# Four PSUM banks for one late feed-forward product, and a pacing copy that holds the cast of a weight chunk instead of its load

## The chip, the cores and the metric

The kernel runs on one core of a Trainium2 chip. The core has five engines with instruction streams of their own: TensorE (PE in the profile) multiplies matrices, VectorE (DVE), ScalarE (ACT) and GpSimd (POOL) work on elements, and SyncE (SP) issues nearly all DMAs here. Each works through its stream in order and waits at semaphores. The metric is the device time of one execution in microseconds, as the median of several runs.

## The reference

One layer of a hybrid decoder on 1024 tokens of width 1024, in float32. Cut to what matters here:

```python
h = rms_norm(x, attn_norm)
z = h @ w_in                          # convolution, q, six k/v groups, gates
conv_out = conv_mixer(a_conv, ...)    # GLU, causal depthwise conv, LayerNorm, swish
nsa_out = nsa_attention(q, kc, vc, ks, vs, kw, vw, gates)   # compressed + selected + window
x = x + concat([conv_out, nsa_out]) @ w_out
h = rms_norm(x, ffn_norm)
gate, up = split(h @ w_gate_up)
x = x + (silu(gate) * up) @ w_down    # width 2816
return rms_norm(x, final_norm)
```

## The kernel before

**Precision.** Every large product is done in three matmuls on fp32r operands. Each float32 operand is split into a rounded high part and the rest; high times high, high times rest and rest times high are added up. For weights this is `load_w` (line 220): a DMA brings a chunk of 512 KB into `w_raw`, ACT casts it into `w_hi` (line 230), and POOL subtracts the two into `w_lo` in four pieces (line 234). There are two buffers for `w_raw` and three each for `w_hi` and `w_lo`, taken in turn. So a load has to wait until POOL has subtracted the chunk two back, and a cast until PE has read the `w_hi` three back for the last time. `Feed` hands the chunks out in order; whoever takes one asks for the one two further on.

**Stages.** The tokens form two sets of 512. First the projections of the first half, the compressed branches and the convolution (to about 210 us). Then attention in two halves ("parts"): in the first (to about 420 us) the queries of the first four token tiles, in the second those of the last four. Attention alone can't fill PE, because each step is a chain: scores on PE (lines 851 to 855, tile `s`), minimum on DVE (859), exponential on ACT (866), the sum's reciprocal on DVE (870, 871, tile `l`), the gating on POOL (876, tile `pr`), a transpose on PE (882, `pt`), its split (240), and the product with the values on PE (910, 911, tile `o`). So `weave` emits a second stream, `fill_all`, between the steps of attention, by a ratio. In the first half this filling is `fill_b`: the second half's projections `zo` (queries and keys), `vo` (values) and `cv` (convolution), all through line 148, with 18 chunks of `w_in`. Then come the output projection of the first set (`wo`, line 1226) and its feed-forward, pair by pair of 128 columns: `gu` (line 1299), the activation `af`, its split `aw`, and `dn` (line 1324), whose sums DVE adds to the residual `x` (line 1327).

After attention, `second` (line 1626) does the same output projection for the second set (line 1250) and its norm, in which POOL scales rows and PE transposes them (line 261). The feed-forward of the first set goes on beside it, again by `weave`. After that the second set's feed-forward runs in a form with fewer products (line 1455).

**What sets the order.** The program emits one stream; a planner then orders each engine's instructions by a simulated time, with the program's order as priority, and adds the semaphores. An instruction that depends on nothing can thus come earlier on its engine than where it is written. Two things hold it:

- *The pace.* With `phase[0] == 0`, that is up to the end of attention's first half, `load_w` lets POOL copy one column of `l` of the attention step `PACE_B = 4` back (list `pace`) into the chunk's own buffer (line 225). What writes that buffer later must wait for the copy, and the copy for that step. In the second half `PACE_C` is 0 and there is no copy.
- *The banks.* The kernel divides PSUM into eight banks of 512 columns: five for the tag `x`, which `s` and `t` share, one for `o`, two for `z`. `next_bank` takes them in turn from a string of tags. The first set's feed-forward uses `FT` (line 1580), a list that holds "z" until `second` has been emitted and `ALL` afterwards (line 1649). It is read anew for each product, so a change takes effect from the next product that is emitted. In `second`, the output projection uses the first six tags of `ALL` ("stostt") and the transposes of the norm use `t`.

The feed-forward product that is emitted beside the norm of `second` is one `down_part`: eight sums of six matmuls each, 3 with the first half of `aw` and 3 with the second.

## Time and profile before

| | |
|---|---|
| median of 3 runs | 1441.14 us (1439.65 to 1441.8) |
| profiled execution | 1443.74 us, span 1442.0 us |
| granted TensorE clock, mean of the span | 0.994 |
| POOL copies of line 225 | 13, from 240.8 to 388.9 us |
| DMA, mean | 136 GB/s |

The span runs from the first to the last instruction; the execution's own time has some 2 us around it. Rows of the profile name an engine, a line of the program, the operation and the tiles (out<-in). Behind the second bar stands the idle time of the engine just before such an instruction, and what ended it. In the table of stretches, each engine's busy time stands beside the stretch's length; PEclk is the clock that TensorE was granted, as a share of full speed. Matmuls overlap: one of 512 columns is shown with some 0.39 us, though the next can start sooner.

### The profile page before, as it was taken

To read this page: it belongs to the slowest core of one execution; us is meant where nothing else is said; L and a number is where in the kernel's file an instruction comes from. 1 tells how busy PE (TensorE), PEld (TensorE's weight loads), DVE (VectorE), ACT (ScalarE), POOL (GpSimd) and SP (SyncE) were. 2 spreads that over 40 slices of the span, in tenths; PEclk is the share of its full clock that TensorE was granted. 3 is DMA by queue.
4 is the path that set the end of the run, shared out by engine and by line. 5 is a ranking of instruction groups with operands and counts; after the bars stand their busy time and mean duration, and the time that the engine had idled before them with its cause. 6 is when DMAs were issued, how large, how long until landed. Compare 5 with 4: busy or idle time off the path is not lost.

```text
span 1442.0 us, 23394 instructions
## 1 busy us (share of the span) xinstructions
PE 1410.9 (98%) x7941; PEld 1224.8 (85%) x7941; DVE 1031.6 (72%) x2306; ACT 763.7 (53%) x1593; POOL 739.4 (51%) x1043
## 2 busy tenths in 40 slices
PE   8999999999999999999999999999999999999997
PEld 7898888977788888888888888887788999999997
DVE  6487786777877859778697875231658987888884
ACT  6333566677865765666756654224325444445443
POOL 6467775766676656666666666546767000000001
PEclk9999999999999999999999999999999999999999
DMA  7246577665777343243343226723235333333421
GB/s 237 76 134 197 171 213 243 194 204 170 203 252 215 88 117 104 83 123 104 95 120 109 79 70 201 225 78 100 74 117 175 118 98 107 88 94 113 116 60 73
DMA packets 234119, 196.13 MB, mean 136 GB/s; under 512 B 13786, under 2 KB 204094, under 8 KB 233999
## 3 DMA queue, kind: packets, MB, share of 16 engines
q1 hardware_dynamic: 233854, 194.41, 44.9%
q8 instruction: 63, 1.03, 0.3%
q14 instruction: 58, 0.47, 0.1%
q10 hardware_dynamic: 144, 0.23, 0.0%
HBM read 160.85 MB, written 33.55 MB: 135 GB/s over the span
## 4 chain that ended last, share of the span: by engine, by line
PE 82%; DMA 5%; DVE 4%; POOL 4%; ACT 3%; issue 1%; SPq 0%; POOLq 0%; ACTq 0%; DVEq 0%
PE gu L1299 18%; PE dn L1324 16%; PE yy L1455 8%; PE pt L882 5%; PE zz L1455 4%; PE vo L148 3%; DMA w_raw<-in_w_in_dram 3%; PE cv L148 3%; PE wo L1250 3%; PE wo L1226 3%; PE o L911 3%; PE o L910 3%; POOL w_lo L234 3%; PE s L851 3%; PE zo L148 2%; PE aa L1455 2%
## 5 line engine op out<-in xcount | busy, mean ns | idle before, releaser
L234 POOL TENSOR_TENSOR w_lo<-w_raw,w_hi 128x256 fp32r<-128x256 f32 (+1 forms) x508 | 410.6, 841 | 169.1 <-ACT w_hi L230 162.5
L1299 PE MATMUL gu<-h,w_hi 128*128 128x512 f32 x768 | 252.5, 397 | 0.0
L1324 PE MATMUL dn<-w_hi,aw 128*128 128x512 f32 x690 | 242.0, 396 | 2.6 <-DVE aw L240 1.3
L230 ACT CAST w_hi<-w_raw 128x1024 fp32r<-128x1024 f32 (+1 forms) x147 | 152.7, 1049 | 171.6 <-PE gu L1299 72.3
L876 POOL TENSOR_SCALAR pr<-pr,l,gates 128x512 f32<-128x512 f32 (+5 forms) x192 | 144.7, 767 | 101.8 <-DVE l L871 86.0
L866 ACT ACTIVATE pr<-pr,m 128x512 f32<-128x512 f32 (+5 forms) x192 | 136.1, 709 | 94.9 <-DVE m L859 56.5
L1299 PEld LDWEIGHTS gu<-h,w_hi 128*128 128x128 f32 x768 | 143.4, 188 | 27.9 <-DVE h L240 0.2
L240 DVE TENSOR_TENSOR pl<-pt,ph 128x384 fp32r<-128x384 f32 x248 | 133.7, 550 | 45.7 <-ACT ph L240 38.7
L1542 POOL TENSOR_TENSOR rs<-rs,mhalf 128x1 f32<-128x1 f32 x4 | 3.3, 832 | 317.3 <-DVE rs L1541 317.2
L1324 PEld LDWEIGHTS dn<-w_hi,aw 128*128 128x128 f32 x690 | 129.3, 188 | 30.3 <-DVE aw L240 2.3
L1299 PE MATMUL gu<-h,w_lo 128*128 128x512 f32 x384 | 152.5, 397 | 0.0
L1327 DVE TENSOR_TENSOR x<-dn,x 128x512 f32<-128x512 f32 x177 | 118.6, 679 | 46.6 <-PE dn L1324 46.2
L240 ACT CAST ph<-pt 128x384 fp32r<-128x384 f32 x248 | 113.5, 474 | 60.7 <-PE pt L882 37.8
L1324 PE MATMUL dn<-w_lo,aw 128*128 128x512 f32 x345 | 136.2, 395 | 0.0
L882 PE MATMUL pt<-ident,pr 128*128 128x128 f32 x744 | 124.7, 274 | 2.5 <-DVE pl L240 1.3
L859 DVE CUSTOM_DVE_ANT_0 pr<-s,base 128x384 f32<-128x384 f32 (+3 forms) x192 | 101.0, 531 | 29.6 <-PE s L855 14.8
L148 PE MATMUL zo<-h,w_hi 128*128 128x512 f32 x320 | 107.7, 404 | 2.8 <-ACT w_hi L230 2.7
L882 PEld LDWEIGHTS pt<-ident,pr 128*128 128x128 f32 x744 | 93.3, 140 | 20.0 <-POOL pr L876 1.9
L1401 ACT CAST w_s<-sum 128x512 fp32r<-128x512 f32 x80 | 49.3, 621 | 113.9 <-PE yy L1455 94.3
L851 PE MATMUL s<-kt,q 128*128 128x384 f32 (+3 forms) x288 | 98.3, 343 | 2.8 <-DVE m L859 2.3
L1455 PEld LDWEIGHTS yy<-term,w_s 128*128 128x128 f32 x720 | 93.4, 188 | 5.4 <-DVE c L1470 0.3
L910 PE MATMUL o<-ph,vt 128*128 128x384 f32 x264 | 95.3, 361 | 1.9 <-DMA vt<-vs_d 0.9
(281 smaller groups left out, 3186.1 us busy)
## 6 DMA issues: line engine op xcount, KB each, us to landing
w_raw<-in_w_gate_up_dram SPq DMA_DIRECT2D x48, 512.0 KB, 3.9
w_raw<-in_w_down_dram SPq DMA_DIRECT2D x43, 512.0 KB, 3.5
w_raw<-in_w_in_dram SPq DMA_DIRECT2D x40, 512.0 KB, 4.6
u_raw<-in_w_gate_up_dram SPq DMA_DIRECT2D x20, 512.0 KB, 4.9
g_raw<-in_w_gate_up_dram SPq DMA_DIRECT2D x19, 512.0 KB, 4.0
q_d<-zh SPq DMA_DIRECT2D x12, 512.0 KB, 5.2
qc<-q_d SPq DMA_DIRECT2D x16, 384.0 KB, 4.6
pc_d<-pct SPq DMA_DIRECT2D x16, 384.0 KB, 3.2
```

What stands on the lines that cost most here:

```text
L148: lastpe[0] = pe.matmul(*args, **kw)
L230: act.copy(hi[:, :n], raw[:, :n])
L234: eng.tensor_sub(lo[:, q], raw[:, q], hi[:, q].bitcast(F32))
L240: pair = act.copy(hi, src), dve.tensor_sub(lo, src, hi.bitcast(F32))
L851: pe.matmul(sv, q2[0], kk_[:, 0, kk], start=True, stop=False)
L866: act.activation(pr[:, c0:n], pr[:, c0:n], AF.Exp, bias=m, scale=-1.0, accum_out=l3[:, r:r + 1])
L876: pool.tensor_scalar(x_, x_, l3[:, r2:r2 + 1], gates[:, i, c:c + 1], op0=ALU.mult, op1=ALU.mult)
L882: pe.transpose(pt[:, r * P:(r + 1) * P], prs[st][1 + r][:, kk * P:(kk + 1) * P], ident)
L910: pe.matmul(o[:, :384], v, ph, start=False, stop=False)
L1299: pe.matmul(o, w[:, k, :], h2[si][h][k // 4][:, k % 4, :], start=n == 0, stop=n == 3 * KT - 1)
L1324: pe.matmul(o, aws[si][:, a, k, t * P:(t + 1) * P], b[:, 0, h], start=n == 0, stop=n == 5)
L1455: pe.matmul(o, w[:, k, :], h[:, k, :], start=fresh and n == 0, stop=n == 11, skip_group_check=not fresh)
```

## The change

In `load_w`, the pacing copy writes a column of `w_hi` instead of `w_raw`. The DMA writes `w_raw`, so it no longer depends on the copy; the cast writes `w_hi`, so now it does. The copy itself no longer waits for `w_raw` to be free but for `w_hi`. In `second`, `FT` gets the tags z, s, z, o between the output projection and the norm, so the feed-forward products that are emitted from there to the end of `second` take their sums from four banks in turn (both of `z`, one of the five of `x`, and `o`) instead of two.

```diff
@@ load_w
         back = PACE_B if phase[0] == 0 else PACE_C
         if len(pace) >= back > 0:
-            pool.tensor_copy(raw[:, 0:1], pace[-back][:, 0:1])
+            pool.tensor_copy(hi[:, 0:1], pace[-back][:, 0:1])
         n = a * b
@@ second
         yield from out_proj_k(Feed(out_loads_k(p), 2), 1, ALL[:6])
+        FT[:] = "zszo"
         set_norm(1, p)
         yield from ffn_norm_in(1, "t", grow)
```

## The prediction

> **What bounds the kernel now.** I read the page first, for the busiest engine, then the stretches, for where that engine is idle, and then who waited for whom inside those stretches.

> ```profile
> span 1442.0 us, 23394 instructions
> ...
> PE 1410.9 (98%) x7941; PEld 1224.8 (85%) x7941; DVE 1031.6 (72%) x2306; ACT 763.7 (53%) x1593; POOL 739.4 (51%) x1043
> ```

> PE is busy for 98% of the span, so a change that leaves PE's work as it is can only win back PE's idle time and the time PE spends at a lower clock. The question is where these lie.

> ```profile
> core 0: us, PE busy (x) PEld busy (x) DVE busy (x) ACT busy (x) POOL busy (x), PEclk, DMA share, GB/s
> 210.00:420.00 210.00, 197.54 (x1143) 171.46 (x1142) 160.13 (x550) 152.19 (x466) 143.16 (x226) 0.97 0.68 210
> 322.00:330.00 8.00, 5.35 (x35) 4.34 (x33) 7.81 (x34) 5.07 (x15) 4.35 (x8) 0.98 0.94 289
> 330.00:337.00 7.00, 6.37 (x23) 5.62 (x24) 2.57 (x14) 5.02 (x21) 4.10 (x7) 0.53 0.31 107
> 382.00:391.00 9.00, 6.89 (x47) 5.88 (x46) 7.86 (x37) 7.21 (x23) 5.60 (x13) 1.00 0.78 219
> 391.00:395.00 4.00, 3.69 (x11) 2.96 (x12) 3.76 (x14) 3.95 (x17) 3.77 (x6) 0.57 0.84 232
> 418.00:422.00 4.00, 4.00 (x13) 3.54 (x13) 1.66 (x6) 1.55 (x5) 3.84 (x7) 0.57 1.07 401
> 420.00:880.00 460.00, 457.11 (x2457) 394.26 (x2456) 353.61 (x888) 283.12 (x524) 295.54 (x425) 1.00 0.40 112
> 1005.00:1023.00 18.00, 16.09 (x82) 12.25 (x81) 12.40 (x19) 10.97 (x17) 13.72 (x11) 1.00 0.11 30
> ```

> Attention's first half (210 to 420 us) has 210.00 − 197.54 = 12.5 us of idle PE; the second half, with twice the length, 2.9 us. Three short stretches show a granted clock of 0.53 to 0.57, and the two that follow a stretch with over 2 us of idle PE (8.00 − 5.35 and 9.00 − 6.89) lie where the change acts. The late feed-forward (1005 to 1023) has 18.00 − 16.09 = 1.9 us of idle. So the two parts of the change sit at the two places where PE still waits.

> Inside attention's first half, the groups by line show what ended PE's idle time:

> ```profile
> L148 PE MATMUL zo<-h,w_hi 128*128 128x512 f32 x112 | 39.5, 415 | 2.7 <-ACT w_hi L230 2.7
> L882 PE MATMUL pt<-ident,pr 128*128 128x128 f32 x186 | 32.7, 280 | 2.4 <-DVE pl L240 1.3 <-DVE m L859 0.4 <-POOL pr L876 0.4
> L851 PE MATMUL s<-kt,q 128*128 128x256 f32 (+3 forms) x79 | 26.2, 335 | 1.3 <-DVE m L859 0.8 <-PE o L910 0.5
> L148 PE MATMUL zo<-h,w_lo 128*128 128x512 f32 x56 | 23.4, 417 | 0.3 <-POOL w_lo L234 0.3
> L911 PE MATMUL o<-pl,vt 128*128 128x384 f32 x60 | 22.1, 368 | 0.5 <-DVE pl L240 0.5
> L910 PE MATMUL o<-ph,vt 128*128 128x384 f32 x60 | 21.7, 362 | 1.8 <-DMA vt<-vs_d 0.9 <-ACT ph L240 0.9
> L148 PE MATMUL cv<-h,w_hi 128*128 128x512 f32 x41 | 14.5, 419 | 1.6 <-ACT w_hi L230 1.6
> ```

> Weights end 2.7 + 0.3 + 1.6 = 4.6 us of it, attention's own steps 2.4 + 1.3 + 0.5 + 1.8 = 6.0 us.

> **The held load.** The copy of line 225 takes `l` of an earlier attention step into the buffer, and what it writes decides what is held.

> ```profile
> L225 POOL COPY w_raw<-l x13: 177/183/188, 240.8 to 388.9; 128x1 f32<-128x1 f32 x13
> ```

> It runs 13 times, so 13 chunks are touched. For two of them the order of time reads, on POOL, in the chain (the load's flight), on ACT and on PE:

> ```profile
> 323.86 0.18 POOL L225 COPY w_raw<-l 128x1 f32<-128x1 f32 x1
> ...
> 324.06 5.39 DMA w_raw<-in_w_in_dram
> ...
> 329.54 1.04 ACT L230 CAST w_hi<-w_raw 128x1024 fp32r<-128x1024 f32 x1 [2.49 <-DMA w_raw<-in_w_in_dram]
> ...
> 330.63 0.79 PE L148 MATMUL zo<-h,w_hi 128*128 128x512 f32 x1 [2.08 <-ACT w_hi L230]
> ```

> ```profile
> 382.71 0.18 POOL L225 COPY w_raw<-l 128x1 f32<-128x1 f32 x1
> ...
> 383.24 4.90 DMA w_raw<-in_w_in_dram
> ...
> 388.21 1.04 ACT L230 CAST w_hi<-w_raw 128x1024 fp32r<-128x1024 f32 x1 [1.44 <-DMA w_raw<-in_w_in_dram]
> ...
> 389.31 0.51 PE L148 MATMUL cv<-h,w_hi 128*128 128x512 f32 x1 [1.62 <-ACT w_hi L230]
> ```

> From copy to cast 329.54 − 323.86 = 5.7 us pass, and 388.21 − 382.71 = 5.5 us; nearly all of it is the load's flight. PE starts the moment the cast has ended.

> Afterwards the copy writes `w_hi`, so the load needs only a free `w_raw`, and the chunk is in the buffer when the copy runs. The cast can follow the copy directly: some 5 us earlier at these two places. The waits were 2.1 and 1.6 us, so both go, and with them the other w_hi and w_lo waits: **−4.6 us** (bounds 0 and −4.6).

> What else the step issues. It has the same 13 copies of 0.18 us, the same DMAs, casts and subtractions. SP's load moves ahead of attention's loads and stores in SP's queue; it then waits there for POOL's subtractions of the chunk two back instead of the copy, which stands behind those on POOL. Its traffic moves to a busy time: one wait for `vt`, 0.9 us, shows what a pushed transfer costs. I take 0, bounds −0.9 and +0.9. One more semaphore hop, from POOL to ACT, is not in the trace; the hop from POOL to SP is (324.06 − 323.86 − 0.18 = 0.02 us), and I take 0 again.

> The copy also gets a wait: for PE's last reading of the `w_hi` that is three chunks old. Queued behind it on POOL stand the gating of line 876 and the subtractions of line 234, for which PE waits. The tightest place before is here (the last matmul of the value chunks, then the copies for the two chunks that take their buffers):

> ```profile
> 268.48 0.29 PE L148 MATMUL vo<-w_hi,h 128*128 128x274 f32 x1
> ...
> 274.57 0.30 POOL L225 COPY w_raw<-l 128x1 f32<-128x1 f32 x2
> ```

> The buffer is free at 268.48 + 0.29 = 268.77, so 274.57 − 268.77 = 5.8 us before POOL gets to the copy. So the wait costs nothing in this order; the planner may choose another.

> **The clock.** The dips at 330 and 391 cost 7.00 × (1 − 0.53) = 3.3 us and 4.00 × (1 − 0.57) = 1.7 us. Each follows the stretch with a weight stall. If that idle time triggers them, they go too: **−5.0 us** (bounds 0 and −5.0). I take the whole, since both follow a weight stall within 2 us; the third dip, at 418, is not counted.
> [...]

> **Four banks.** For the product of the late feed-forward that runs beside the second set's norm, `FT` is "z", two PSUM banks. After the change products rotate over z, s, z, o: four.

> ```profile
> PE dn L1324 <- DVE aw L240: 1.1, 1, 1.1
> PE dn L1324 <- DVE x L1327: 0.5, 1, 0.5
> PE dn L1324 <- DVE rs L248: 0.2, 1, 0.2
> ...
> 1005.45 0.39 PE L1324 MATMUL dn<-w_hi,aw 128*128 128x512 f32 x1
> ...
> 1008.42 2.31 DVE L240 TENSOR_TENSOR aw<-af,aw 128x512 fp32r<-128x512 f32 x1 [1.88 <-ACT aw L240]
> ...
> 1010.78 0.50 PE L1324 MATMUL dn<-w_hi,aw 128*128 128x512 f32 x1 [1.14 <-DVE aw L240]
> ...
> 1023.31 22.26 PE gu L1299 x96
> ```

> A product is six matmuls, five of which don't need the late half of `aw` (DVE's, done at 1008.42 + 2.31 = 1010.73). With two banks PE has ten such matmuls; with four, twenty. One takes 22.26 / 96 = 0.232 us, so 10 more fill 2.3 us and cover the 1.1 us. The wait for `x` is for a bank whose sum DVE hasn't added yet; with two more banks it goes, and the 0.2 us too: **−1.8 us** (bounds 0 and −1.9, the stretch's whole idle time). The transposes of the norm share s's five buffers; the product takes at most one of them at a time, and I cost that at 0. Without that cover it is about one such 0.5 us wait. DVE does the same adds. Next late is the norm's own chain, which PE meets only at transposes, between feed-forward matmuls.

> **What is late next.** When weights come early, PE reaches attention's steps sooner, and their waits of 6.0 us can grow. At worst they take all 4.6 us; at best none, since earlier weights also give PE work while attention isn't ready. I take half, **+2.3 us**.

> **Sum.** −4.6 − 5.0 − 1.8 + 2.3 = −9.1 us. The profiled execution took 1443.74 us (span 1442.0), so it would take 1434.6. It lies 2.6 us above the median shown, 1441.14; from the median the forecast is **1432.0 us**. Its own range: with nothing given back and the `vt` wait saved 1441.14 − 11.4 − 0.9 = 1428.8; with all 4.6 us given back and one more `vt` wait 1441.14 − 6.8 + 0.9 = 1435.2.

> **The rivals.**
> *The dips stay.* The clock falls for another reason, or the idle time that remains suffices. The third dip stands behind a wait that isn't for weights:

> ```profile
> 417.25 0.74 PE L1226 MATMUL wo<-w_hi,mix 128*128 128x512 f32 x2 [1.86 <-DMA mix<-mix_d]
> ```

> For it speaks that 12.5 − 4.6 = 7.9 us of idle remain; against it that two of three dips stand behind a weight stall. Then −9.1 + 5.0 = −4.1: 1437.0 us. Chance 0.18. [...]
> *Attention takes over.* The first half runs at the pace of attention's softmax, of which the copies are the beat; weights that come sooner change only what PE waits for, and the clock falls as before. For: 6.0 us of waits there against 4.6. Against: PE is busy for 94% of that half and finds other work. Only −1.8 is left: 1439.3 us. Chance 0.20.
> *The load isn't early.* SP, in order, comes to it no sooner, because it stands behind waiting loads of attention, so the cast still follows a late landing. Again 1439.3 us. Against: the buffer of the load of 324.06 was free over 20 us earlier, when POOL had subtracted the chunk two back:

> ```profile
> 297.18 2.83 POOL L234 TENSOR_TENSOR w_lo<-w_raw,w_hi 128x256 fp32r<-128x256 f32 x4
> ```

> Chance 0.06.
> *POOL is held, and it is slower.* The planner moves the copy forward on POOL by more than the 5.8 us, or PE is that much later there than planned; POOL then stands in front of the gating, and PE waits for transposes. One such stall priced like the one at 330 is 2.1 + 3.3 = 5.4 us. It decides once POOL holds PE as long as weights do now (9.6 us with the dips, so nothing is won there) and one stall more: 5.4 − 1.8 = +3.6, 1444.7 us. For: the new order isn't known, and the copy's new wait stands on the engine that serves both attention and the weights. Against: 5.8 us is the tightest place of the 13. Chance 0.14.

> **How the numbers follow.** The forecast has 0.42. A measurement of this kernel can tell 0.2%, 2.9 us, from no change. Faster by more: the forecast 0.42, two thirds of the dips' case (its 4.1 us is little above 2.9) 0.12, and a quarter of the two 1439.3 cases 0.06: 0.60. Slower by more: the POOL case, 0.14, and 0.02 of the rest, 0.16. Same: 0.24. The range leaves out half of the POOL case and as much at the fast end: 1428 to 1444.

> **What would show it.** Right: line 225's group reads `w_hi<-l`; the casts follow it within 1 us; waits of zo and cv for w_hi are gone from PE's list; the granted clock in the stretches after 322 and 382 is 1.00; the late product's waits for `aw` and `x` are gone. Wrong: casts that still end with a wait for the DMA (the load isn't early); POOL's idle time before line 225 ended by PE (POOL held); the same idle sum in 210 to 420 under other names (attention takes over); dips without weight stalls.

## The result and the profile after

The changed kernel takes 1431.33 us (median of 4 runs, 1430.44 to 1432.28) against 1441.47 us of the kernel before in the same session (4 runs): 0.9934 [0.9916, 0.9952], 10.1 us less. Taken once more in a later session, under the label changed_again, it took 1428.43 us (6 runs) against 1441.76 (26 runs): 0.9915 [0.9897, 0.9933]. The forecast was 1432.0 us, with a range from 1428 to 1444.

The head of the page and the stretches that the prediction showed, now of the changed kernel (columns as there; at the end of a line the granted clock, the DMA share and GB/s):

```profile
span 1430.6 us, 23380 instructions
...
PE 1406.5 (98%) x7941; PEld 1224.0 (86%) x7941; DVE 1030.7 (72%) x2306; ACT 762.7 (53%) x1593; POOL 738.6 (52%) x1043
```

```profile
210.00:420.00 210.00, 203.09 (x1184) 177.57 (x1183) 165.10 (x566) 154.48 (x475) 145.84 (x229) 0.98 0.73 225
322.00:330.00 8.00, 7.65 (x45) 6.55 (x46) 7.77 (x31) 5.49 (x16) 7.50 (x12) 1.00 0.87 282
330.00:337.00 7.00, 7.00 (x45) 6.14 (x44) 5.14 (x22) 6.15 (x27) 4.21 (x8) 1.00 0.41 114
382.00:391.00 9.00, 9.00 (x52) 7.91 (x51) 8.47 (x27) 7.82 (x27) 7.13 (x12) 1.00 0.70 216
391.00:395.00 4.00, 4.00 (x22) 3.38 (x21) 3.88 (x13) 3.93 (x12) 4.00 (x7) 1.00 0.40 89
239.00:243.00 4.00, 3.96 (x15) 3.86 (x16) 2.38 (x10) 3.21 (x12) 4.00 (x10) 0.57 0.48 179
409.00:414.00 5.00, 5.00 (x16) 4.04 (x17) 3.37 (x9) 2.57 (x7) 3.74 (x6) 0.66 1.06 408
420.00:880.00 460.00, 457.08 (x2458) 393.81 (x2457) 353.78 (x890) 283.72 (x523) 298.60 (x427) 1.00 0.39 109
1005.00:1023.00 18.00, 18.00 (x92) 14.94 (x91) 12.10 (x18) 8.02 (x11) 12.00 (x13) 1.00 0.28 80
```

PE's idle time in attention's first half fell from 12.5 to 210.00 − 203.09 = 6.9 us, and in the late product from 1.9 to nothing. The second half is as it was (2.9 us). The dips at 330 and 391 are gone. There is a new one at 239, and the one of 418 is now at 409.

The groups of PE in the same first half (matmuls by line and tile; behind the second bar the idle time before them):

```profile
L148 PE MATMUL zo<-h,w_hi 128*128 128x512 f32 x141 | 46.8, 400 | 0.2 <-ACT w_hi L230 0.2
L882 PE MATMUL pt<-ident,pr 128*128 128x128 f32 x213 | 36.1, 276 | 0.8 <-DVE m L859 0.4 <-POOL pr L876 0.2
L851 PE MATMUL s<-kt,q 128*128 128x128 f32 (+3 forms) x95 | 31.9, 344 | 0.6 <-DVE pl L240 0.5
...
L911 PE MATMUL o<-pl,vt 128*128 128x384 f32 x69 | 25.4, 368 | 0.3 <-DVE pl L240 0.3
L910 PE MATMUL o<-ph,vt 128*128 128x384 f32 x69 | 24.8, 359 | 1.0 <-ACT ph L240 0.9
L148 PE MATMUL cv<-h,w_hi 128*128 128x512 f32 x64 | 21.3, 399 | 0.0
...
L1226 PE MATMUL wo<-w_hi,mix 128*128 128x512 f32 x27 | 10.3, 436 | 2.4 <-DMA mix<-mix_d 2.4
...
L905 PE MATMUL o<-pct,vcs 128*128 128x384 f32 x15 | 5.9, 396 | 1.4 <-DVE ou L915 1.4
```

Waits for weights: 4.6 us before, 0.2 now. Attention's own waits: 6.0 us before; now 0.8 + 0.6 + 0.3 + 1.0 and a new 1.4 at line 905, 4.1 us. The wait for `mix`, which the change doesn't touch, went from 1.9 to 2.4 us.

Why weights are no longer late, in the order of time (SP's queue, then POOL, ACT and PE), for the first of the two chunks that the prediction followed:

```profile
295.40 0.55 SPq L229 DMA_DIRECT2D w_raw<-in_w_in_dram  x1
```

```profile
324.25 0.18 POOL L225 CAST w_hi<-l 128x1 fp32r<-128x1 f32 x1
324.66 1.05 ACT L230 CAST w_hi<-w_raw 128x1024 fp32r<-128x1024 f32 x1
...
325.77 0.49 PE L148 MATMUL zo<-h,w_hi 128*128 128x512 f32 x1 [0.23 <-ACT w_hi L230]
```

Its load is issued 28.9 us ahead of the copy. The cast follows the copy by 0.4 us instead of 5.7, and PE waits 0.23 us instead of 2.08.

**Where the time went, stretch by stretch.** Idle time and clock don't add up to time by themselves, so I also compared the traces matmul by matmul: the n-th matmul of each line and tile in one against the n-th of the same in the other, and the median difference of their starts in a stretch of 40 us. Negative is earlier than in the profiled execution of the kernel before:

```
us, against before       from 160   from 440   from 960  from 1040   at the end
changed kernel               +0.6       -8.3       -8.3      -11.4        -11.5
the same, later session      +0.2      -12.2      -12.2      -15.3        -15.3
```

From 160 to 440 us, that is across attention's first half, the changed kernel gains 8.9 us. Idle time makes 12.5 − 6.9 = 5.6 of it. The clock makes 3.3: three dips before lost 3.3 + 1.7 + 1.7 = 6.7, two dips now lose 4.00 × (1 − 0.57) = 1.7 and 5.00 × (1 − 0.66) = 1.7. Together 8.9; that the two add up to the tenth is chance, since a stall can cost more than the idle time shown, as in the late product below (1.31 us for 1.14). The second half neither gains nor loses, and the late product brings 3.1.

### The profile page after: what moved, and what is told of

It is laid out like the page before. It is cut to its first block, busy times and chain, and to the rows that moved or that the text cites. A ratio compares the mean times of both kernels' runs of the same rounds, so it can differ in the third digit from the quotient of the medians.

```text
span 1430.6 us, 23380 instructions
## 1 busy us (share of the span) xinstructions
PE 1406.5 (98%) x7941; PEld 1224.0 (86%) x7941; DVE 1030.7 (72%) x2306; ACT 762.7 (53%) x1593; POOL 738.6 (52%) x1043
## 4 chain that ended last, share of the span: by engine, by line
PE 89%; DVE 4%; DMA 3%; POOL 2%; ACT 2%; issue 1%; SPq 0%; POOLq 0%; ACTq 0%; DVEq 0%
PE gu L1299 19%; PE dn L1324 17%; PE yy L1455 8%; PE zo L148 6%; PE pt L882 5%; PE zz L1455 4%; PE vo L148 3%; PE zc L148 3%; PE wo L1250 3%; PE wo L1226 3%; PE o L911 3%; PE o L910 3%; PE s L851 3%; PE cv L148 2%; PE aa L1455 2%; PE s L855 2%
## 5 line engine op out<-in xcount | busy, mean ns | idle before, releaser
L234 POOL TENSOR_TENSOR w_lo<-w_raw,w_hi 128x256 fp32r<-128x256 f32 (+1 forms) x508 | 409.9, 839 | 157.4 <-ACT w_hi L230 152.2
L1299 PE MATMUL gu<-h,w_hi 128*128 128x512 f32 x768 | 253.1, 397 | 0.0
L1324 PE MATMUL dn<-w_hi,aw 128*128 128x512 f32 x690 | 240.9, 395 | 0.7 <-DVE af L1306 0.3
L230 ACT CAST w_hi<-w_raw 128x1024 fp32r<-128x1024 f32 (+1 forms) x147 | 152.5, 1050 | 163.4 <-PE gu L1299 61.1
L876 POOL TENSOR_SCALAR pr<-pr,l,gates 128x512 f32<-128x512 f32 (+5 forms) x192 | 144.8, 767 | 97.1 <-DVE l L871 86.9
L240 DVE TENSOR_TENSOR pl<-pt,ph 128x384 fp32r<-128x384 f32 x248 | 133.4, 549 | 52.9 <-ACT ph L240 44.5
L1299 PEld LDWEIGHTS gu<-h,w_hi 128*128 128x128 f32 x768 | 143.4, 188 | 27.7 <-DVE h L240 0.2
L1324 PEld LDWEIGHTS dn<-w_hi,aw 128*128 128x128 f32 x690 | 129.4, 188 | 27.2 <-DVE af L1306 0.9
L1299 PE MATMUL gu<-h,w_lo 128*128 128x512 f32 x384 | 152.5, 397 | 0.0
L1327 DVE TENSOR_TENSOR x<-dn,x 128x512 f32<-128x512 f32 x177 | 118.3, 679 | 47.2 <-PE dn L1324 46.7
L240 ACT CAST ph<-pt 128x384 fp32r<-128x384 f32 x248 | 112.9, 474 | 53.3 <-PE pt L882 29.4
L1324 PE MATMUL dn<-w_lo,aw 128*128 128x512 f32 x345 | 136.2, 395 | 0.0
L882 PE MATMUL pt<-ident,pr 128*128 128x128 f32 x744 | 123.9, 273 | 0.9 <-DVE m L859 0.4
L859 DVE CUSTOM_DVE_ANT_0 pr<-s,base 128x384 f32<-128x384 f32 (+3 forms) x192 | 100.7, 530 | 22.3 <-PE s L853 14.3
L882 PEld LDWEIGHTS pt<-ident,pr 128*128 128x128 f32 x744 | 93.5, 140 | 17.7 <-issue 1.3
L148 PE MATMUL zo<-h,w_hi 128*128 128x512 f32 x320 | 105.6, 399 | 0.5 <-DVE pct L720 0.3
L851 PE MATMUL s<-kt,q 128*128 128x384 f32 (+3 forms) x288 | 98.7, 346 | 2.1 <-DVE m L859 1.5
L911 PE MATMUL o<-pl,vt 128*128 128x384 f32 x264 | 94.8, 359 | 0.9 <-DVE pl L240 0.9
```

Of the source, the lines that this page charges most:

```text
L148: lastpe[0] = pe.matmul(*args, **kw)
L230: act.copy(hi[:, :n], raw[:, :n])
L234: eng.tensor_sub(lo[:, q], raw[:, q], hi[:, q].bitcast(F32))
L240: pair = act.copy(hi, src), dve.tensor_sub(lo, src, hi.bitcast(F32))
L851: pe.matmul(sv, q2[0], kk_[:, 0, kk], start=True, stop=False)
L876: pool.tensor_scalar(x_, x_, l3[:, r2:r2 + 1], gates[:, i, c:c + 1], op0=ALU.mult, op1=ALU.mult)
```

## The experiments

The changed line and the line of the banks can be set one at a time, and the pace can be moved. Three readings of the gain in attention's first half were set against each other:

- **A, earlier is better.** PE gains because weights reach it sooner. Whatever releases the casts still earlier gains more, whatever releases them later loses.
- **B, ACT.** A cast that waits on ACT for its landing load holds attention's exponentials and splits behind it in ACT's stream; the gain is ACT's time.
- **C, the flight.** The copy set the right moment, but the load's flight (5.39 and 4.90 us in the prediction's two rows) stood between it and PE. What takes the flight out of that path gains, whichever tile is held.

In the list of waits from 235 to 396 us, ACT's rows for the held casts and for attention's exponential read, before and in the changed kernel (us, times, the longest):

```profile
ACT w_hi L230 <- DMA w_raw<-in_w_in_dram: 10.9, 7, 3.4
ACT pr L866 <- DVE m L859: 9.5, 15, 2.3
```

```profile
ACT pr L866 <- DVE m L859: 18.5, 19, 2.6
...
ACT w_hi L230 <- DMA w_raw<-in_w_in_dram: 2.2, 1, 2.2
...
ACT w_hi L230 <- POOL w_hi L225: 1.5, 2, 0.8
```

ACT stands at the casts for 2.2 + 1.5 = 3.7 us instead of 10.9, but 9.0 us longer in front of the exponential, for DVE's minimum. All waits in that list add up to 38.5 and 35.2 us, so on the whole ACT was freed by little.

All kernels were compared with the kernel before in their own session (medians 1440.96, 1441.76 and 1441.83 us, 25 to 29 runs each). "In place" is the gain from 160 to 960 us in the comparison by matmuls; that profile of the kernel before lies about 2 us above its median, which makes these some 2 us too good. The last two columns are PE's idle time in that one profile: from 210 to 420 us, attention's first half, and from 420 to 880 us, where no copy runs in any of them. In the kernel before they are 12.5 and 2.9 us, in the changed kernel's first profile 6.9 and 2.9.

```
                                       us      ratio [95%]             in place  idle 1st  2nd
cast alone                          1436.44   0.9966 [0.9952, 0.9979]    -6.7      8.0     3.2
banks alone                         1439.92   0.9994 [0.9977, 1.001]     +0.8     13.4     2.5
load held, a step earlier           1437.09   0.9975 [0.996,  0.9989]    -5.6      8.2     4.5
cast held, a step later  (3 back)   1430.4    0.993  [0.9909, 0.9952]   -10.3      7.0     3.2
cast held, two later     (2 back)   1444.12   1.0016 [1.0003, 1.0029]    +2.8     13.6     4.4
cast held, a step earlier (5 back)  1451.61   1.0057 [1.0032, 1.0082]   +12.1     19.8     3.8
nothing held                        1446.88   1.0032 [1.0016, 1.0049]    +4.0      7.9    10.7
both held, load one step earlier    1438.25   0.997  [0.9958, 0.9983]    -2.8      7.9     4.9
both held, load two steps earlier   1436.32   0.9955 [0.9939, 0.9971]    -2.7      8.2     6.4
first two chunks not held           1439.94   0.9985 [0.997,  1.0001]    -2.7     12.4     2.9
changed kernel, again               1428.43   0.9915 [0.9897, 0.9933]   -12.4      6.1     2.9
```

### The parts alone

```diff
 cast_alone, against the changed kernel
-        FT[:] = "zszo"
 banks_alone, against the kernel before
+        FT[:] = "zszo"
```

> Only the pacing copy is changed (it writes w_hi); the late feed-forward keeps its two z banks. Theory A (what counts is how early a chunk's weights are ready against attention's progress): the whole gain but the banks' share, the measured 0.66% of the changed kernel less 1.8 us of idle time, so 7 to 8 us faster than before; the stretch around 1000 to 1020 us again shows 1.5 to 2 us of idle PE. Rival (the gain comes from the late product, and the first half only swaps its waits): under 3 us.

> Only FT is set to z, s, z, o; the copy still writes w_raw. Theory A: the first half of attention is as before (12.5 us of idle PE from 210 to 420 us, 4.6 us of it for weights), the late product's 1.8 us of waits are gone: 1.5 to 2 us faster than before. Rival as above: 5 us or more.

The cast alone brings 4.9 us (0.9966 of 1441 us; the interval, 0.9952 to 0.9979, is 6.9 to 3.0 us), less than the 7 to 8 that A expected. The banks alone can't be told from no change by the time: −0.9 us [−3.3, +1.4]. In place they can. In the comparison by matmuls, the step from 960 to 1040 us is −3.08 us for banks_alone, and −3.07 or −3.08 in all eleven profiles of this study with four banks; for cast_alone, the only other one with two, it is 0.00. So the banks are worth 3.1 us, more than the 1.5 to 2 expected, and scatter elsewhere can hide it: at 960 us, ahead of anything that the banks touch, banks_alone stood 2.4 us behind the kernel before in these two executions.

The stretches of the late product in cast_alone and in banks_alone show the idle time of it:

```profile
1000.00:1023.00 23.00, 21.32 (x105) 16.86 (x106) 16.50 (x22) 11.13 (x17) 18.72 (x17) 1.00 0.16 47
```

```profile
1000.00:1023.00 23.00, 23.00 (x109) 18.91 (x108) 12.11 (x20) 12.17 (x19) 17.32 (x16) 1.00 0.19 55
```

In the kernel before the idle time of this stretch is 1.9 us, but the gain is 3.1. The starts of matmuls tell why:

```profile
1009.24 0.40 PE L1324 MATMUL dn<-w_lo,aw 128*128 128x512 f32 x1
1010.78 0.73 PE L1324 MATMUL dn<-w_hi,aw 128*128 128x512 f32 x2 [1.14 <-DVE aw L240]
```

From one start to the next 1.54 us pass where 0.23 would do, so this stall costs 1.31 us; the profile gives 1.14 as idle, since the matmul before it is shown as busy for its whole 0.40 us. The matmul behind this stall also took 0.34 us until the next one started (1010.78 to 1011.12), instead of 0.23. Added up over the starts from 998 to 1026 us that lie more than 0.30 us apart, what exceeds 0.23 us comes to 3.1 us in the kernel before and to 0.2 in banks_alone.

cast_alone has the changed kernel's instruction order up to 1000 us, too. Its profile stands within 0.9 us of the changed kernel's up to 650 us, and then loses 2.1 us at one late minimum of attention, which the changed kernel's profile doesn't show:

```profile
655.59 0.55 PE L882 MATMUL pt<-ident,pr 128*128 128x128 f32 x3 [0.88 <-DVE m L859]
```

The two parts thus add up to 4.9 + 3.1 = 8.0 us, against 10.1 and 13.3 for the whole change. What is missing to the first lies within the intervals. What is missing to the second doesn't quite: by the ratios it is 12.2 ± 2.6 us against 4.9 ± 1.9 and 3.1. A stall in one profile can't explain a median of twelve runs, so the cause of the rest stays open. The changed kernel's own two profiles stand 3.9 us apart from 410 us on.

### The load a step earlier, the cast a step later

```diff
 load_5, against the changed kernel
-PACE_B = 4
+PACE_B = 5
-            pool.tensor_copy(hi[:, 0:1], pace[-back][:, 0:1])
+            pool.tensor_copy(raw[:, 0:1], pace[-back][:, 0:1])
 cast_3, against the changed kernel
-PACE_B = 4
+PACE_B = 3
```

> The copy writes w_raw again, so it holds the load, but takes the column of five attention steps back instead of four (PACE_B = 5), with the four banks. A step of the first half lasts some 200/32 = 6.2 us, about the 5.5 us that the load takes from copy to cast. Theory A: weights are ready about as early as in the changed kernel, so 7 to 10 us faster than before, with under 1.5 us of PE waits for w_hi. Theory B (the gain comes from ACT no longer standing still for a landing, 10.9 us before, with softmax queued behind it): ACT still waits 8 to 12 us for DMAs, and the time is within 4 us of before.

> The changed kernel with PACE_B = 3: the cast is held, but by an attention step one later. Theory A: weights are ready some 6 us later, about as late as before the change; PE waits 3 to 6 us for weights again, and only the banks and little more are left: 1 to 4 us faster than before. Theory B: ACT waits for no landing here either, so 7 to 10 us faster.

load_5 leaves the flight where it was and only moves it one step of attention ahead. It gains 3.9 us of which the banks are 3.1, and ACT still stands at seven casts:

```profile
ACT w_hi L230 <- DMA w_raw<-in_w_in_dram: 8.0, 7, 3.1
```

By its time alone that is B's forecast. The stretches say where the time lies, attention's first half and the second:

```profile
210.00:420.00 210.00, 201.82 (x1183) 175.90 (x1183) 163.35 (x562) 155.48 (x473) 144.39 (x228) 0.99 0.71 221
420.00:880.00 460.00, 455.49 (x2447) 391.27 (x2446) 357.25 (x888) 283.54 (x527) 294.64 (x426) 1.00 0.38 108
```

In the first half PE's idle time fell to 8.2 us, most of the way to the changed kernel's, with one dip in place of three; in the comparison by matmuls load_5 gains 9.0 us from 160 to 440 us, the changed kernel 8.9. It falls behind in the second half, where no copy runs, with 4.5 us of idle against 2.9 and 3.4 us lost from 440 to 960 us. So where the copy acts, a load released one step earlier did about as well in this execution as taking the flight out of the way, while ACT still waits 8.0 us at casts against 10.9. That speaks against B, and it doesn't tell A from C.

cast_3 frees its casts later than the changed kernel, the 13 copies by 3 to 12 us (6 in the middle), and is just as fast: 0.993 against 0.9934 and 0.9915. PE waits 1.8 us for its weights from 235 to 396 us, where A expected 3 to 6. None of its casts waits for anything:

```profile
L230 ACT CAST w_hi<-w_raw 128x1024 fp32r<-128x1024 f32 (+1 forms) x14 | 14.6, 1051 | 0.0
```

A falls here: with the flight out of the way, later by a step loses nothing.

### How much hold, and the changed kernel again

```diff
 no_pace, cast_2 and cast_5, against the changed kernel
-PACE_B = 4
+PACE_B = 0      (2, 5)
 both_held, and both_2 with 2 for 1
+        if len(pace) >= back + 1 > 1:
+            pool.tensor_copy(raw[:, 0:1], pace[-back - 1][:, 0:1])
 free_first
-        if len(pace) >= back > 0:
+        if len(pace) > back + 2 > 2:
```

> The changed kernel with PACE_B = 0: no copy at all, neither the load nor the cast is held. Theory C (what cost time is that the load's flight lay between the copy and the cast, where ACT, POOL and PE stand in a planned order and meet a landing later than planned): the flight is out of the path here too, ACT waits under 4 us for landings of w_in, PE under 1 us for weights; within 4 us of the changed kernel. Theory A (the earlier the weights the better) wants it at least as fast as the changed one. Rival (the hold itself is worth something, because it spreads the projections over attention's steps): 5 us or more slower than the changed kernel, with attention's waits on PE up.

> The changed kernel with PACE_B = 2: the cast is held by two steps more than in the changed kernel, some 12 us. Theory C: lateness alone does no harm as long as the planner knows it, since PE's order puts attention first; within 4 us of the changed kernel, ACT's waits for landings near 0. Theory A: weights are 6 us later than before the change, PE waits over 5 us for them, slower than before or like it.

> The changed kernel with a second copy: w_hi is held by the column of four steps back as in the changed kernel, and w_raw by that of five steps back. The load is late again, by all but one step of some 6 us, but the flight of about 5 us is still covered. Theory C: as fast as the changed kernel within 3 us, ACT's waits for landings of w_in under 4 us. Rival D (what helps is that SP can send the loads far ahead, freeing its queue): most of the gain is lost, 3 to 6 us slower than the changed kernel.

> The changed kernel, measured beside the following ones. 8 to 11 us faster than before; its time is what the other three are compared with.

Without any hold the kernel is slower than before. Its weights are never late, but PE takes the projections too early and has too few left at the end of the half, where attention's chain is alone:

```profile
420.00:460.00 40.00, 31.63 (x161) 24.66 (x162) 33.91 (x127) 30.04 (x90) 21.06 (x30) 0.90 0.60 170
```

8.4 of the 10.7 us in the table's last column stand there; the changed kernel has none (40.00 of 40.00 busy). So the hold itself is worth 1446.88 − 1428.43 = 18.5 us (both from one session), as the rival said. This is the second blow to A, and C's forecast, within 4 us of the changed kernel, fails with it. The changed kernel itself gained 13.3 us here, somewhat more than the 8 to 11 expected. cast_2, with the casts two steps later, is slower than before as well, 15.7 us behind the changed kernel where C allowed 4. PE waits for weights only 0.8 us from 235 to 396 us, where A expected over 5; 10.9 us it waits there for attention's steps and loads. That the late casts leave it too little to do beside them fits this, but no run shows it by itself.

both_held lets the load go one step ahead of the cast instead of at will. ACT's waits for loads are then 5.6 us (10.9 before), and it gains 3.5 us, about what the banks bring, so it is 9.8 us slower than the changed kernel, where C allowed 3. That a load is only a step ahead is not enough to cover it.

> As both_held, but w_raw is held by the column of six steps back, two before that of the cast. Some 12 us lie between, where in both_held six of the pairs of copies were under 5 us apart. Theory C (the landing between copy and cast is what costs): ACT's waits for landings of w_in under 3 us, within 3 us of the changed kernel. Rival D (the loads must be free altogether, or what both_held lost it lost by its other order in the second half): again 6 to 10 us slower than the changed kernel, with those waits under 3 us all the same.

> The changed kernel with PACE_B = 5: the cast is held by an attention step one earlier. Theory A (the earlier the better): 1 to 3 us faster than the changed kernel. From the kernel without a copy, which was 18 us slower than the changed one because PE had no projections left at the end of the first half (8.4 us of idle PE from 420 to 460 us): slower by 0 to 5 us than the changed kernel.

> The changed kernel, but the first two chunks (the value weights) are not held; the other 11 are. In the changed kernel PE stands still for 2.1 us between 235.7 and 238.4 us with these weights not yet cast, and the clock is 0.5 for 3.4 us behind it. If the hold of these two is what starves PE there: that stall gone, 2 to 4 us faster than the changed kernel. Rival (the hold is worth something for every chunk, as the kernel without any showed): the stall comes back later, 0 to 5 us slower than the changed kernel.

With two steps ahead the flight is covered:

```profile
ACT w_hi L232 <- DMA w_raw<-in_w_in_dram: 1.0, 1, 1.0
```

and PE waits for no weights in that stretch. By B and by C this kernel should be as fast as the changed one. It is 5 to 8 us slower (0.9955 against 0.9934 and 0.9915; the intervals overlap with the first, not with the second). Both halves of attention again:

```profile
210.00:420.00 210.00, 201.78 (x1172) 177.04 (x1171) 164.37 (x559) 152.96 (x469) 146.57 (x241) 0.98 0.70 218
420.00:880.00 460.00, 453.56 (x2438) 391.71 (x2438) 357.01 (x883) 283.87 (x524) 291.22 (x424) 1.00 0.38 109
```

In the first half its idle time, 8.2 us, is 1.3 to 2.1 us above the changed kernel's two profiles; in the second it is 6.4 us against 2.9, where neither a load nor a cast is held. So in this execution the larger part of what it lacks lies where the change doesn't act, as one form of rival D had it; both_held shows the same, with 7.9 and 4.9 us.

cast_5 is the clearest miss. It differs from the changed kernel by one step, and it is 20 to 23 us slower by the medians (18 to 20 by the ratios). PE's waits (from 235 to 396 us):

```profile
PE o L905 <- DVE ou L915: 4.6, 2, 2.6
PE zo L148 <- ACT w_hi L230: 2.7, 2, 2.1
PE o L910 <- ACT ph L240: 1.7, 3, 0.9
PE s L855 <- DMA kt<-ks_d: 1.6, 1, 1.6
```

PE waits 12.4 us for attention's own steps and loads there (15.1 in all, of which weights are 2.7), more than three times the changed kernel's 3.4. POOL is not the cause: no idle time stands before its copies.

```profile
L225 POOL CAST w_hi<-l 128x1 fp32r<-128x1 f32 x12 | 2.1, 188 | 0.0
```

free_first leaves the two value chunks at 241 us without a hold, because PE stands still in front of them in the changed kernel (4.00 − 2.50 = 1.5 us of idle from 235 to 239 us; the three waits there are for DVE, ACT and POOL, none for a weight). It should have won 2 to 4 us and came out 9 to 12 slower. In place of that stall it has

```profile
PE s L851 <- DVE m L859: 5.9, 3, 5.3
```

one of 5.3 us, for a minimum of attention that DVE had not done.

What also sets these kernels apart from the changed one is the order. Each edit makes the planner order each engine anew: of PE's 7941 matmuls, compared place by place in the traces, 760 are of another line or tile in the changed kernel than in the kernel before, and 2532 differ between the changed kernel and cast_3. My reading is that where such an order puts too little beside one step of attention, PE stalls there, whatever the weights do; the stalls above fit it, but no run changes the order alone. None of these kernels is clearly faster than the changed one; cast_3 equals it.

## Why the prediction was right

The time was forecast within a microsecond, and its mechanism stood: line 225's group reads `w_hi<-l`, 13 times, the loads run ahead but for one, and nothing in attention's first half waits for weights but 0.2 us. That it came within a microsecond is in part luck: three of the four terms were off by 1.3 to 4.2 us, on both sides, and the later session's 1428.43 us lies 3.6 us below the forecast, still in the range.

- **The waits for weights, −4.6.** Right: 4.6 to 0.2 us.
- **POOL's copy is not held.** Right. The answer for line 225 has no idle time in front of any of the 13 copies:

```profile
L225 POOL CAST w_hi<-l x13: 173/185/194, 241.4 to 385.6; 128x1 fp32r<-128x1 f32 x13
its engine sat idle before it (us, times) until:
who waited for it (us, times):
```

- **The casts follow within 1 us.** Half right. Six of the 13 start within 1 us of the copy's start; six more follow by 1 to 3.4 us, and one by 11.5 (copy at 243.26, cast at 254.76), since its load was issued only at 250.72: SP had stood for 11.9 us in front of a store of `mix_d` that waited for ACT. ACT stands idle for the load for 2.2 us.
- **The clock, −5.0.** The two dips went, but one came at 239, so it brought 3.3 in the profile. Over the timed runs of both (80 of the kernel before in the later sessions, 10 of the changed one) the mean granted clock is 0.9959 and 0.9974; that is 1442 × 0.0041 − 1431 × 0.0026 = 2.2 us (an estimate that takes time to be lost in proportion to the clock). In the 3.41 us ahead of each of these two PE was idle for 1.6 and 2.2 us, of which waits for weights were 1.1 and 1.6 (3.41 us is the length of a dip; the last section compares such pieces), so their going with the waits fits the prediction's condition, which no run shows by itself. The term was too large because it let dips only go. The stall that the new dip follows stood in the kernel before as well, with 4.00 − 2.45 = 1.6 us of idle and no dip after it:

```profile
239.00:243.00 4.00, 3.85 (x25) 3.31 (x24) 3.14 (x13) 2.96 (x10) 3.75 (x9) 1.00 0.50 120
235.00:239.00 4.00, 2.45 (x16) 1.78 (x15) 3.43 (x18) 3.80 (x16) 1.02 (x3) 1.00 0.46 154
```

- **What is late next, +2.3.** Wrong in its sign. The step let attention's own waits grow by half of what the weights gave up; they fell from 6.0 to 4.1 us. Of these 1.9 us, 0.9 is the wait for the load of `vt`, which the prediction had priced at nothing either way and which didn't come back. For the rest, ACT's shorter stand at casts (3.7 us instead of 10.9) with attention's work behind it would be an explanation, but no run shows that alone: both_2 has ACT's waits for loads gone too (1.0 us) and PE's waits for attention's steps and loads at 6.4 us.
- **The banks, −1.8.** Right in kind; the size is 3.1, because the term counted idle time, and the stall there cost more than the idle time that is shown (1.31 us for 1.14).

In sum: −4.6 − 5.0 + 2.3 − 1.8 = −9.1 was forecast; −4.4 for weights, −1.9 for attention's steps, +0.5 for `mix` and +0.2 for small groups make the first half's 5.6 us of idle, −3.3 the clock and −3.1 the banks: −12.0 between two profiled executions, −10.1 and −13.3 in the medians. The clock was priced too high, what is late next and the banks too low, so the total came out closer than its terms.

Of the rivals, *the dips stay* was half seen: two dips in place of three, and neither follows a wait for weights, which the prediction named as a sign of being wrong. *The load isn't early* was seen in one of the 13 chunks, the one with the load at 250.72. *Attention takes over* and *POOL is held* were not, though cast_5 and free_first show what the first of these looks like when it happens.

**What stays open.** That the flight stood in PE's way is shown by the rows of the two chunks and by the waits and the two dips that went. How much of the gain in attention's first half is due to it and how much to the order that the planner happened to make isn't. C forecast the time of four kernels (nothing held, casts two steps later, both held in two ways) as that of the changed one, and all four are slower; both_2 covers the flight and gains 5.5 us, of which the banks are 3.1; load_5 leaves the flight in and does about as well in the first half; and one step of the pace moves the time by 20 us. An experiment would have to hold the order and change the flight alone. That wasn't tried.

## What to carry to other kernels

Where a load is held back to keep weights from coming too early, hold the first step after the load, if a buffer is free: the same moment of release then costs a cast (1.05 us here) and not a flight (5.39 and 4.90 us here). Here that change alone brought 4.9 us. Price a stall of PE by the distance of starts (1.31 us in the late product), not by the idle time (1.14). And where a planner orders the code, one good setting is no proof of its reason: take the neighbours (here 2, 3, 4 and 5 steps: 1444, 1430, 1428 to 1431 and 1452 us) before believing a slope.

## What the hardware showed that was not expected

- **The same stall, with and without a dip.** The wait for `mix` at about 408 us stands in both profiles of the changed kernel, which have the same code. In the stretch from 396 to 414 us, first the one of the result, then the later one:

```profile
396.00:414.00 18.00, 15.29 (x71) 12.21 (x70) 12.24 (x36) 11.07 (x32) 16.58 (x25) 0.91 1.01 338
```

```profile
396.00:414.00 18.00, 16.05 (x88) 13.40 (x87) 13.66 (x39) 12.16 (x31) 16.72 (x24) 1.00 1.01 354
```

  2.7 us of idle with a dip, 2.0 without; the comparison by matmuls puts 2.0 us between the two executions there. The dips last 3.41 us, the one at 330 in the kernel before 6.83. The granted clock in them is 0.50:

```profile
239.40:242.80 3.40, 3.40 (x13) 3.30 (x13) 2.18 (x9) 2.61 (x8) 3.40 (x10) 0.50 0.45 170
```

  Matmuls slow down with it: in the dip at 410 the six starts of 512 columns from 410.72 to 412.86 us lie 0.43 us apart; from 409.28 to 409.97 us, ahead of it, they lie 0.23 apart.

```profile
387.72:391.13 3.41, 1.21 (x5) 0.84 (x5) 2.30 (x6) 2.88 (x7) 3.20 (x7) 1.00 0.80 231
```

```profile
406.66:410.08 3.42, 1.14 (x5) 0.97 (x6) 2.41 (x6) 3.35 (x8) 3.42 (x6) 1.00 1.09 366
```

```profile
402.93:406.34 3.41, 1.75 (x10) 1.09 (x8) 1.68 (x6) 2.81 (x6) 3.41 (x7) 1.00 1.09 361
406.34:409.75 3.41, 3.13 (x14) 2.60 (x15) 2.08 (x5) 2.21 (x6) 2.90 (x5) 1.00 1.06 397
```

  With a dip, 2.2 and 2.3 us of idle PE fell into one piece; without, 1.7 and 0.3 into two. From 210 to 1400 us, outside the dips, the pieces with the most idle time hold 2.2, 1.9 and 1.6 us in the kernel before (from 387.72, 415.03 and 326.28 us) and 2.3 and 1.55 us in the changed one (from 406.66 and 236.00), and a dip follows each of the five. The next hold 1.4 us in both (from 493.53 and 485.17), and none follows. The amount alone doesn't tell: the later profile's piece with 1.7 us has no dip behind it, the one from 236.00 us has. That stall is cut in the kernel before into 1.0 and 0.5 us, without a dip.

  So a stall of some 1.5 to 3 us came with a dip in one execution and without in another. That this depends on where the pieces lie, which differs between the two executions of the changed kernel (dips at 239.41 and 239.09 us), is my reading of these few cases; no run shows it by itself.
